# Squares of the low-rank inputs summed tile by tile, rotary tables made in the linear attention, x fetched ahead of the second weights

## The chip, the core and the metric

One core of a Trainium2 chip runs the whole kernel. Its engines are TensorE (PE, with PEld for the loading of its stationary operand), VectorE (DVE), ScalarE (ACT), GpSimd (POOL) and SyncE (SP), which issues most transfers. The metric is the device time of one execution in microseconds, the median of several runs. Smaller is better.

## The reference

A decoder block on x of 1024 tokens by 1024 channels, in float32. One normalised input feeds one wide projection; its parts go to two branches, multi-head latent attention (8 heads, rotary part of 32 channels) and gated linear attention (4 heads, chunks), which are gated, merged and projected back.

```python
h = rmsnorm(x, g_in[l])
proj = h @ w_in[l]
(c_q, c_kv, k_r, z_mla, q_g, k_g, v_g, a_lr, z_gla, gate_mla, gate_gla) = jnp.split(proj, split_points, axis=-1)
q = (rmsnorm(c_q, g_q[l]) @ w_uq[l]).reshape(B, S, MLA_HEADS, MLA_QK)
q = jnp.concatenate([q[..., :MLA_NOPE], apply_rope(q[..., MLA_NOPE:], cos, sin)], axis=-1)
kv = (rmsnorm(c_kv, g_kv[l]) @ w_ukv[l]).reshape(B, S, MLA_HEADS, MLA_NOPE + MLA_VDIM)
k_rope = apply_rope(k_r[:, :, None, :], cos, sin)
o_mla = mla_attention(q, k, v_mla).reshape(B, S, MLA_WIDTH)
log_a = jax.nn.log_sigmoid((a_lr @ w_gla_gate[l] + b_gla_gate[l]).astype(jnp.float32)) / GLA_GATE_NORM
o_gla = gla_chunked(q_g, k_g, v_g, log_a)
merged = jax.nn.sigmoid(gate_mla) * y_mla + jax.nn.sigmoid(gate_gla) * y_gla
x = x + merged @ w_out[l]
return rmsnorm(x, g_final)
```

The low-rank inputs are c_kv (256 channels, two tiles of 128) and c_q (384, three tiles). Their normalisation needs the sum of the squares over all channels of each token. The rotary tables are the sines and cosines of position times frequency.

## The kernel before

The tokens are done in two halves of 512. A half goes through four stages: the start with the low-rank inputs (the latent stage), the linear attention, the latent attention, and the merge with the output products. To keep float32 accuracy each operand is split in a high and a low part, and each product of tiles is three matmuls: high by high, high by low, low by high.

The weights of a half are a stream of units (class Stream). A unit is one tile of 128 output columns: 24 matmuls of 128 x 128 by 128 x 512, written as a generator that yields behind each six. For each unit a weight of 512 KB is loaded (load_raw, two buffers), cast to its high part by ScalarE, and its low part is made by VectorE or GpSimd (split_raw, three buffers each). ahead() loads LOAD_AHEAD = 2 weights and splits SPLIT_AHEAD = 3 ahead of use. step(n) advances the stream by n yields; upto(name) runs it through a unit; ride(chain) runs other work and advances the stream by what that work yields, so that matmuls of units lie between its steps. The units of a half begin with misc (the gate's rank-16 input and the rotary key), ckv0, ckv1, cq0, cq1, cq2, then q0, k0, v0, z0, z1 and so on for four heads.

The order of each engine's instructions is made by a planner from a simulated run: what stands first in the code has precedence, but an engine that is idle gets any later instruction whose inputs and buffers are ready. Transfers on SyncE's queue are ordered in the same way, and at run time an engine takes its instructions strictly in the planned order.

The start of the first half (h == 0): eleven products of zeros (NWARM, tile zw), the first weight in two pieces, x tile 0, then st.ahead() (the next weights), then the prologue's x tiles 1 to 3 (xs, each 512 KB with two k-tiles: xh by ScalarE, xl by VectorE), the constants, and x again by rows (xr), whose squares ScalarE sums for the row scales rcol (POOL makes the power, L252). bcast_row (L257) turns a column of scales into a row by eight small matmuls.

In the latent stage four chains lie over the units. decay() makes the gate: stk from krr, four products with wgs (L693) into two banks, on each an Abs of ScalarE (L694) and a minimum of VectorE (L695), then Exp and Ln over all, then sums along the tokens with the row rst. latent() for ckv and cq: each latent unit ends with a square into csq and a copy into craw (L326, L327); when all tiles are there, matmuls of two columns with one2 add the squares over the channels (L715, 8 for ckv and 12 for cq in each half, two records each in the trace), and from these come the scales. tables() (L665 to L680) makes the sines and cosines into um[:, 2:4], and rotate(krr, ...) turns the rotary key (L627 to L630). In the code tables() stands behind unit cq2 and the rotation behind latent_q. csq has a single buffer, as has each of the banks tr, at and ups; ops has two, and the units' results three.

## Time and profile before

| | us |
|---|---|
| median of 3 runs (1082.48 to 1083.81) | 1083.74 |
| the profiled execution | 1085.81 |
| its span in the trace | 1084.0 |
| outside the span | 1.81 |
| TensorE busy, share of the span | 1048.3, 97% |
| VectorE, ScalarE, GpSimd busy | 714.0, 542.1, 374.9 |
| granted clock of TensorE, mean | 0.98 |

The page's chain of work that ended last gives TensorE 77% of the span, VectorE 12%, ScalarE 4%. Matmuls are pipelined: a product of 512 columns is shown with some 0.4 us, while the next one starts earlier, so a busy TensorE need not be one at its best; the spacing of starts and the granted clock tell that. The granted clock is 1.00 at 2.4 GHz and 0.50 at 1.2 GHz. In the waits, the name behind the arrow is the instruction that came last.

### The profile page before, as it was taken

Reading aid. Unit: us, or ns where it says so; the run is one execution under the profiler, and the core shown is the slowest. Engines: PE = TensorE matmul, PEld = TensorE weight load, DVE = VectorE, ACT = ScalarE, POOL = GpSimd, SP = SyncE. Lnnn points to the kernel's source line nnn. Section 1 sums busy time; section 2 is a strip of 40 time slices with the busy share of each in tenths; the row PEclk is TensorE's granted clock in tenths of the full one; section 3 lists DMA queues with packets and bytes.
Section 4 is the critical chain, followed back from the end, with each engine's and each line's share of the span. In section 5 each row is a group of like instructions: output and inputs, shape, how many; then the busy total and the mean of one; then the engine's idle time right before and its main releaser. Section 6 shows DMA issues by size and latency. Waiting matters only on the chain.

```text
span 1084.0 us, 14078 instructions
## 1 busy us (share of the span) xinstructions
PE 1048.3 (97%) x5231; PEld 872.4 (80%) x5231; DVE 714.0 (66%) x1114; ACT 542.1 (50%) x910; POOL 374.9 (35%) x274
## 2 busy tenths in 40 slices
PE   8999999999999989999999999999999998999997
PEld 5798998987778867888889989988777776788875
DVE  5796555557586776466887655455767877667673
ACT  5744334455556653444574444344664656553232
POOL 2361121114445542230524211104454656533420
PEclk8899999999999999999999999999999999899999
DMA  8213213235433446644412233235422223424532
GB/s 297 98 59 97 97 60 117 97 100 195 139 98 111 144 139 250 226 138 144 165 60 78 78 102 101 80 112 158 122 96 70 81 83 121 125 90 161 175 111 98
DMA packets 46118, 132.05 MB, mean 122 GB/s; under 512 B 5232, under 2 KB 7664, under 8 KB 45920
## 3 DMA queue, kind: packets, MB, share of 16 engines
q1 hardware_dynamic: 37760, 113.96, 32.1%
q0 software_dynamic: 3680, 8.78, 3.0%
q10 hardware_dynamic: 4608, 8.39, 2.1%
q8 instruction: 41, 0.67, 0.3%
q14 instruction: 29, 0.24, 0.1%
HBM read 110.01 MB, written 21.10 MB: 121 GB/s over the span
## 4 chain that ended last, share of the span: by engine, by line
PE 77%; DVE 12%; ACT 4%; issue 2%; DMA 2%; POOL 1%; SPq 0%; POOLq 0%; DVEq 0%; ACTq 0%
PE pj L201 58%; DVE pl L943 2%; PE y L548 2%; PE y L546 2%; PE y L547 2%; PE ops L201 2%; DVE mx L893 1%; PE sc L930 1%; PE sc L932 1%; PE sc L933 1%; PE ov L951 1%; PE ov L952 1%; PE sc L886 1%; PE at L201 1%; DVE wlo L188 1%
## 5 line engine op out<-in xcount | busy, mean ns | idle before, releaser
L201 PE MATMUL pj<-xl,whi 128*128 128x512 f32 x800 | 301.0, 399 | 1.4 <-DVE xl L282 1.4
L201 PE MATMUL pj<-xh,whi 128*128 128x512 f32 x672 | 270.5, 403 | 2.4 <-ACT whi L187 1.6
L187 ACT CAST whi<-wraw 128x1024 fp32r<-128x1024 f32 (+1 forms) x151 | 155.3, 1029 | 122.0 <-PE pj L201 91.3
L201 PEld LDWEIGHTS pj<-xl,whi 128*128 128x128 f32 x800 | 153.5, 192 | 31.9 <-DVE xl L282 2.9
L201 PE MATMUL pj<-xh,wlo 128*128 128x512 f32 x672 | 176.6, 397 | 0.0
L188 POOL TENSOR_TENSOR wlo<-wraw,whi 128x1024 fp32r<-128x1024 f32 (+2 forms) x52 | 118.2, 2274 | 140.8 <-ACT whi L187 67.4
L201 PEld LDWEIGHTS pj<-xh,whi 128*128 128x128 f32 x672 | 129.7, 193 | 28.0 <-ACT whi L187 1.9
L201 PEld LDWEIGHTS pj<-xh,wlo 128*128 128x128 f32 x672 | 127.2, 191 | 26.3
L188 DVE TENSOR_TENSOR wlo<-wraw,whi 128x1024 fp32r<-128x1024 f32 x100 | 127.4, 1275 | 21.5 <-ACT whi L187 21.3
L945 POOL TENSOR_TENSOR acc<-acc,p 128x512 f32<-128x512 f32 (+3 forms) x80 | 84.9, 1061 | 86.0 <-ACT p L939 70.5
L943 DVE TENSOR_TENSOR pl<-p,ph 128x512 fp32r<-128x512 f32 (+3 forms) x80 | 70.3, 886 | 23.4 <-ACT ph L942 23.2
L939 ACT ACTIVATE p<-sc 128x512 f32<-128x512 f32 (+3 forms) x80 | 37.3, 468 | 68.8 <-DVE sc L935 50.8
L201 PE MATMUL pj<-wlo,xh 128*128 128x256 f32 x256 | 64.4, 285 | 0.0
L201 PE MATMUL pj<-whi,xh 128*128 128x256 f32 x256 | 64.2, 284 | 0.0
L893 DVE TENSOR_REDUCE mx<-sc 128x1 f32<-128x512 f32 (+2 forms) x96 | 51.8, 551 | 11.6 <-PE sc L886 10.4
L548 PE MATMUL y<-whi,zl 128*128 128x512 f32 x128 | 50.5, 396 | 0.5 <-DVE zl L211 0.5
L547 PE MATMUL y<-wlo,zh 128*128 128x512 f32 x128 | 50.4, 395 | 0.0
L546 PE MATMUL y<-whi,zh 128*128 128x512 f32 x128 | 49.5, 396 | 0.0
L201 PEld LDWEIGHTS pj<-wlo,xh 128*128 128x128 f32 x256 | 49.0, 191 | 0.3
L201 PEld LDWEIGHTS pj<-whi,xh 128*128 128x128 f32 x256 | 48.9, 191 | 0.3
L211 POOL TENSOR_TENSOR ql<-qi,qh 128x512 fp32r<-128x512 f32 x8 | 12.4, 1554 | 93.5 <-ACT qh L210 93.5
L349 DVE TENSOR_TENSOR zr<-pj,rbc 128x512 f32<-128x512 f32 x32 | 22.0, 688 | 33.8 <-PE pj L201 33.5
(298 smaller groups left out, 2101.6 us busy)
## 6 DMA issues: line engine op xcount, KB each, us to landing
wraw<-in_dram SPq DMA_DIRECT2D x141, 512.0 KB, 3.5
gtd<-zr ACTq DMA_DIRECT2D x32, 256.0 KB, 2.2
zr<-gtd SPq DMA_DIRECT2D x32, 256.0 KB, 2.9
xr<-in_dram SPq DMA_DIRECT2D x8, 512.0 KB, 9.4
ugd<-uo SPq DMA_DIRECT2D x16, 256.0 KB, 2.2
...
```

The costliest lines, as they stand in the source:

```text
L187: nc.scalar.copy(out=hi[:, 0:n], in_=raw[:, 0:n])
L188: getattr(nc, lo_engine).tensor_tensor(out=lo[:, 0:n], in0=raw[:, 0:n], in1=R(hi[:, 0:n]), op=ALU.subtract)
L201: nc.tensor.matmul(out=ps, lhsT=a, rhs=b, start=(i == 0), stop=(i == 3 * n - 1))
L211: (lo_engine or nc.vector).tensor_tensor(out=lo, in0=src, in1=R(hi), op=ALU.subtract)
L349: nc.vector.tensor_tensor(out=zr, in0=c.ps, in1=c.rbc, op=ALU.mult)
L546: nc.tensor.matmul(out=c.ops[t], lhsT=a[0], rhs=b[0], start=(k == 0), stop=False)
L547: nc.tensor.matmul(out=c.ops[t], lhsT=a[0], rhs=b[1], start=False, stop=False)
L548: nc.tensor.matmul(out=c.ops[t], lhsT=a[1], rhs=b[0], start=False, stop=(k == 7))
L893: nc.vector.reduce_max(mx[:, t, b:b + 1], ps[:, 0:n], axis=mybir.AxisListType.X)
L939: nc.scalar.activation(p[:, 0:n], ps[:, 0:n], AF.Exp, scale=SCALE)
L943: nc.vector.tensor_tensor(out=pl[:, 0:n], in0=p[:, 0:n], in1=R(ph[:, 0:n]), op=ALU.subtract)
L945: nc.gpsimd.tensor_tensor(out=s.acc[:, q0:TH], in0=s.acc[:, q0:TH], in1=p[:, 0:n], op=ALU.add)
```

## The change

Five things are changed. (1) The matmuls that add squares (four for each tile) are now put in a list, and issued tile by tile within the next latent unit, behind 18 of its 24 products; what is left is issued in latent(). ckv's sums use the bank ups, cq's the bank at. (2) tables() is a generator; its steps and the rotation of krr are taken one at each yield of the first three heads' linear attention. Its buffers are now parts of um. (3) In the first half's start only the first weight is split, x tiles 1 and 2 are fetched, and then the next weights follow. (4) In unit misc of the first half six products of zeros, of 512 columns, stand behind the fourth, sixth, ... fourteenth product. (5) wgs and rst lie in the pool of the linear attention: wgs is written to memory in the first half and read back in the second, rst is loaded in each half; the raw constants share one buffer.

```diff
--- before.py
+++ after.py
@@ -214,13 +214,15 @@
     vecs = mk(cst, [P, NVEC], F32, "vecs")
     nc.sync.dma_start(out=vecs, in_=vec)
 
+    def move(out, in_, queue=None):
+
+        (queue or nc.sync).dma_start(out=out.bitcast(F32), in_=in_.bitcast(F32))
+
     def vcol(base, i=0):
         return vecs[:, base + i:base + i + 1]
 
     idn = mk(cst, [P, P], F32, "idn")
     idr = mk(cst, [P, P], F32R, "idr")
-    wgs = mk(cst, [P, 512], F32R, "wgs")
-    rst = mk(cst, [P, TH], F32, "rst")
     msk = mk(cst, [P, 3, P], F32, "msk")
     onh = mk(cst, [P, 256], F32R, "onh")
     spr = mk(cst, [48, 4, P], F32R, "spr")
@@ -238,6 +240,7 @@
     junk = mk(cst, [P, 512], BF16, "junk")
     gst = [mk(cst, [P, 256], F32, f"gst{g}") for g in range(4)]
 
+    wgd = dram.tile([96, 512], F32R, tag="wgd", name="wgd")
     ugd = dram.tile([8, P, TH], F32, tag="ugd", name="ugd")
     gtd = dram.tile([16, P, TH], F32, tag="gtd", name="gtd")
     vsp = dram.tile([P, 4, HEADS, P], F32R, tag="vsp", name="vsp")
@@ -311,20 +314,49 @@
 
         @unit("misc", wunit(U_MISC), "vector")
         def _(w):
-            yield from proj(c, w)
+            if h == 0:
+                c.ps = mk(pj, [P, TH], F32, "pj")
+                todo = []
+                for k in range(KT):
+                    todo += [(w[0][:, k, :], c.xh[:, k, :]), (w[0][:, k, :], c.xl[:, k, :])]
+                todo += [(w[1][:, k, :], c.xh[:, k, :]) for k in range(KT)]
+                for i, (a, b) in enumerate(todo):
+                    mm = nc.tensor.matmul(out=c.ps, lhsT=a, rhs=b, start=(i == 0), stop=(i == 23))
+                    if i % 2 == 1 and 1 < i < 14:
+                        with tc.issue_after(mm.ins):
+                            nc.tensor.matmul(out=c.zp, lhsT=c.zw[:, 0:P], rhs=c.zw, start=True, stop=True)
+                    if i % 6 == 5 and i < 23:
+                        yield
+            else:
+                yield from proj(c, w)
             c.misc = c.ps
 
-        c.craw = {}
+        c.craw, c.cps, c.sums = {}, {}, {"ckv": [], "cq": []}
 
         def latent_unit(tag, i, u0):
             @unit(f"{tag}{i}", wunit(u0 + i), "gpsimd")
             def _(w):
-                yield from proj(c, w)
+                for n, _ in enumerate(proj(c, w)):
+                    if n == 2:
+                        for todo in c.sums.values():
+                            while todo:
+                                todo.pop(0)()
+                    yield
                 if i == 0:
-                    c.craw[tag] = (mk(c.pp, [P, 3, TH], F32, "craw" + tag), mk(c.pp, [P, 3, TH], F32, "csq"))
+                    c.craw[tag] = (mk(c.pp, [P, 2 if tag == "ckv" else 3, TH], F32, "craw" + tag), mk(c.pp, [P, 3, TH], F32, "csq"))
                 raw, sq = c.craw[tag]
                 nc.scalar.activation(sq[:, i, :], c.ps, AF.Square)
                 nc.scalar.copy(out=raw[:, i, :], in_=c.ps)
+
+                def add():
+                    if i == 0:
+                        c.cps[tag] = mk(c.gps, [P, TH], F32, "at" if tag == "cq" else "ups")
+                    last = i == (1 if tag == "ckv" else 2)
+                    for t in range(4):
+                        nc.tensor.matmul(out=c.cps[tag][:, 2 * t:2 * t + 2], lhsT=sq[:, i, t * P:(t + 1) * P], rhs=one2,
+                                         start=(i == 0 and t == 0), stop=last, skip_group_check=True)
+
+                c.sums[tag].append(add)
 
         for i in range(2):
             latent_unit("ckv", i, U_CKV)
@@ -590,22 +622,22 @@
         st.fences |= {f"{h}{u}" for u in ("misc", "uqr", "hi0", "hi1", "hi2", "hi3", "yg0", "ym0", "wo00")}
 
 
-    def consts(bp):
+    def consts(bp, wgs):
         graw = mk(bp, [P, 512], F32, "graw")
         nc.sync.dma_start(out=idn, in_=idn_d)
         nc.sync.dma_start(out=graw[0:96], in_=wgate)
         nc.scalar.copy(out=wgs[0:96, :], in_=graw[0:96])
         nc.vector.tensor_tensor(out=wgs[64:96, :], in0=graw[64:96], in1=R(wgs[64:96, :]), op=ALU.subtract)
+        move(wgd, wgs[0:96])
         nc.vector.tensor_scalar(out=ggh, in0=vecs[:, V_GGLA:V_GGLA + 2], scalar1=0.5, scalar2=None, op0=ALU.mult)
 
     def consts2(bp):
-        nc.sync.dma_start(out=rst, in_=rst_d)
         nc.sync.dma_start(out=msk, in_=msk_d)
         nc.vector.tensor_copy(out=idr, in_=idn)
-        oraw = mk(bp, [P, 256], F32, "onraw")
+        oraw = mk(bp, [P, 512], F32, "graw")[:, 0:256]
         nc.sync.dma_start(out=oraw, in_=onh_d)
         nc.vector.tensor_copy(out=onh, in_=oraw)
-        sraw = mk(bp, [48, 4, P], F32, "sraw")
+        sraw = mk(bp, [P, 512], F32, "graw")[0:48].rearrange("p (a b) -> p a b", a=4)
         nc.sync.dma_start(out=sraw, in_=spread_d)
         nc.vector.tensor_copy(out=spr, in_=sraw)
 
@@ -616,14 +648,40 @@
         gs = hs.enter_context(ExitStack())
         c.gp = gp = pool("gla", 1, stack=gs)
         c.gp2 = gp2 = pool("gla2", 2, stack=gs)
-        gps = pool("glaps", 1, PSUM, stack=gs)
+        c.gps = gps = pool("glaps", 1, PSUM, stack=gs)
+        wgs = mk(gp, [P, 512], F32R, "wgs")
+        rst = mk(gp, [P, TH], F32, "rst")
         um = mk(up, [P, 4, TH], F32, "um")
         sn, cn = um[:, 2, :], um[:, 3, :]
         krr = mk(up, [P, TH], F32, "krr")
 
-        def rotate(raw, rows):
-
-            sw = mk(c.pp, [P, TH], F32, "sw")
+        def tables():
+
+            ang, pi, tn = um[:, 0, :], um[:, 1, :].bitcast(I32), cn
+            nc.sync.dma_start(out=pi, in_=pos[:, h * TH:(h + 1) * TH].broadcast_to([P, TH]))
+            yield
+            nc.vector.tensor_copy(out=ang, in_=pi)
+            nc.vector.tensor_scalar(out=ang, in0=ang, scalar1=vcol(V_FREQ), scalar2=None, op0=ALU.mult)
+            yield
+            nc.vector.tensor_scalar(out=tn, in0=ang, scalar1=INV2PI, scalar2=MAGIC, op0=ALU.mult, op1=ALU.add)
+            nc.vector.tensor_scalar(out=tn, in0=tn, scalar1=MAGIC, scalar2=None, op0=ALU.subtract)
+            yield
+            for cc in (C1, C2, C3):
+                nc.vector.scalar_tensor_tensor(out=ang, in0=tn, scalar=-cc, in1=ang, op0=ALU.mult, op1=ALU.add)
+                yield
+            nc.vector.tensor_scalar(out=ang, in0=ang, scalar1=PI_CLAMP, scalar2=-PI_CLAMP, op0=ALU.min, op1=ALU.max)
+            nc.vector.scalar_tensor_tensor(out=tn, in0=ang, scalar=-1.0, in1=ang, op0=ALU.mult, op1=ALU.max)
+            yield
+            nc.scalar.activation(sn, ang, AF.Sin, scale=vcol(V_SGN))
+            nc.scalar.activation(cn, tn, AF.Sin, scale=-1.0, bias=hpi)
+            yield
+            rotate(krr, slice(96, 128), um[:, 1, :])
+            yield
+
+        def rotate(raw, rows, sw=None):
+
+            if sw is None:
+                sw = mk(c.pp, [P, TH], F32, "sw")
             nc.vector.stream_shuffle(out=sw[rows], in_=raw[rows], mask=[(i + 16) % 32 for i in range(32)])
             nc.vector.tensor_tensor(out=sw[rows], in0=sw[rows], in1=sn[rows], op=ALU.mult)
             nc.vector.tensor_tensor(out=raw[rows], in0=raw[rows], in1=cn[rows], op=ALU.mult)
@@ -636,9 +694,9 @@
             if h == 0:
                 with ExitStack() as bs:
                     bp = pool("boot", 1, stack=bs)
-                    zw = mk(bp, [P, TH], BF16, "zw")
+                    c.zw = zw = mk(gp, [P, TH], BF16, "zw")
                     nc.vector.memset(zw, 0.0)
-                    zp = mk(gps, [P, TH], F32, "tr")
+                    c.zp = zp = mk(gps, [P, TH], F32, "tr")
                     for _ in range(NWARM):
                         nc.tensor.matmul(out=zp, lhsT=zw[:, 0:P], rhs=zw, start=True, stop=True)
                     pro = prologue(0, bp, 4)
@@ -646,38 +704,26 @@
                     st.nload = 1
                     next(pro)
                     load_rest(st.raw[0], st.specs[0][0])
-                    for _ in range(NB):
+                    st.LOAD_AHEAD, st.SPLIT_AHEAD = 0, 1
+                    st.ahead()
+                    st.LOAD_AHEAD, st.SPLIT_AHEAD = Stream.LOAD_AHEAD, Stream.SPLIT_AHEAD
+                    for _ in range(3):
                         next(pro)
                     st.ahead()
-                    for _ in range(4 - NB):
-                        next(pro)
-                    consts(bp)
+                    next(pro)
+                    consts(bp, wgs)
                     for _ in pro:
                         pass
                     consts2(bp)
+            if h == 1:
+                move(wgs[0:96], wgd)
+            nc.sync.dma_start(out=rst, in_=rst_d)
             c.pp = pp = pool("start", 1, stack=ss)
             st.upto(f"{h}misc")
             st.step(NBS[h])
             bps = mk(gps, [P, TH], F32, "tr")
             bcast_row(c.rcol, c.rbc, bps)
             nc.vector.tensor_tensor(out=krr, in0=c.misc, in1=c.rbc, op=ALU.mult)
-
-            def tables():
-
-                pi = mk(pp, [P, TH], I32, "pi")
-                nc.sync.dma_start(out=pi, in_=pos[:, h * TH:(h + 1) * TH].broadcast_to([P, TH]))
-                ang = mk(pp, [P, TH], F32, "ang")
-                nc.vector.tensor_copy(out=ang, in_=pi)
-                nc.vector.tensor_scalar(out=ang, in0=ang, scalar1=vcol(V_FREQ), scalar2=None, op0=ALU.mult)
-                tn = mk(pp, [P, TH], F32, "tn")
-                nc.vector.tensor_scalar(out=tn, in0=ang, scalar1=INV2PI, scalar2=MAGIC, op0=ALU.mult, op1=ALU.add)
-                nc.vector.tensor_scalar(out=tn, in0=tn, scalar1=MAGIC, scalar2=None, op0=ALU.subtract)
-                for cc in (C1, C2, C3):
-                    nc.vector.scalar_tensor_tensor(out=ang, in0=tn, scalar=-cc, in1=ang, op0=ALU.mult, op1=ALU.add)
-                nc.vector.tensor_scalar(out=ang, in0=ang, scalar1=PI_CLAMP, scalar2=-PI_CLAMP, op0=ALU.min, op1=ALU.max)
-                nc.vector.scalar_tensor_tensor(out=tn, in0=ang, scalar=-1.0, in1=ang, op0=ALU.mult, op1=ALU.max)
-                nc.scalar.activation(sn, ang, AF.Sin, scale=vcol(V_SGN))
-                nc.scalar.activation(cn, tn, AF.Sin, scale=-1.0, bias=hpi)
 
             def decay():
 
@@ -709,11 +755,10 @@
                 hi = mk(lat, [P, n, TH], F32R, "chi" + tag)
                 lo = mk(lat, [P, n, TH], F32R, "clo" + tag)
                 yield 3
-                cps = mk(gps, [P, TH], F32, "at")
-                for t in range(4):
-                    for i in range(n):
-                        nc.tensor.matmul(out=cps[:, 2 * t:2 * t + 2], lhsT=sq[:, i, t * P:(t + 1) * P], rhs=one2,
-                                         start=(i == 0), stop=(i == n - 1))
+                full = "c" + ("kv" if tag == "k" else "q")
+                while c.sums[full]:
+                    c.sums[full].pop(0)()
+                cps = c.cps[full]
                 f1 = mk(pp, [P, 4], F32, "f1" + tag)
                 nc.vector.tensor_tensor(out=f1, in0=c.rcol, in1=c.rcol, op=ALU.mult)
                 f2 = mk(pp, [P, 4], F32, "f2" + tag)
@@ -741,9 +786,7 @@
             st.upto(f"{h}ckv1")
             st.ride(latent_kv())
             st.upto(f"{h}cq2")
-            tables()
             st.ride(latent_q())
-            rotate(krr, slice(96, 128))
 
 
         with ExitStack() as gs2:
@@ -834,9 +877,15 @@
                     nc.sync.dma_start(out=ugd[f], in_=uo)
                     yield 1
 
+            side = tables()
             for g in range(4):
                 st.upto(f"{h}v{g}")
-                st.ride(core(g))
+                for n in core(g):
+                    st.step(n)
+                    if g < 3:
+                        next(side, None)
+            for _ in side:
+                pass
         gs.close()
```

## Rows read from the trace of the kernel before

**Rows 1.** Windows: busy us (instructions) of each engine, then granted clock, DMA share, GB/s.
```profile
6.00:10.90 4.90, 2.74 (x8) 1.38 (x9) 2.94 (x5) 2.57 (x5) 0.98 (x1) 1.00 0.92 359
...
10.90:17.75 6.85, 6.01 (x14) 4.23 (x14) 6.08 (x8) 5.86 (x10) 1.40 (x1) 0.50 1.04 371
...
41.60:48.50 6.90, 6.32 (x17) 5.16 (x18) 4.07 (x8) 5.47 (x7) 1.02 (x1) 0.51 0.42 152
...
62.10:65.50 3.40, 3.40 (x10) 2.62 (x9) 3.40 (x5) 0.21 (x2) 2.74 (x2) 0.50 0.29 113
...
80.00:120.00 40.00, 40.00 (x250) 35.94 (x249) 24.20 (x40) 17.13 (x35) 8.57 (x7) 1.00 0.24 79
...
560.90:563.90 3.00, 1.97 (x18) 1.92 (x18) 3.00 (x7) 3.00 (x7) 0.89 (x1) 1.00 0.00 0
...
563.90:570.70 6.80, 6.80 (x20) 5.45 (x20) 6.49 (x11) 2.46 (x6) 5.69 (x5) 0.50 0.24 80
```

**Rows 2.** Timeline of TensorE, start: start us, us, engine, line, instruction, [wait before].
```profile
1.30 3.91 PE L643 MATMUL tr<-zw 128*128 128x512 bf16 x11 [1.30 <-DVE zw L640]
...
9.89 0.50 PE L201 MATMUL pj<-xh,whi 128*128 128x512 f32 x1 [1.55 <-ACT whi L187]
...
12.90 0.79 PE L201 MATMUL pj<-xl,whi 128*128 128x512 f32 x1 [0.84 <-DVE xl L282]
...
23.93 1.05 PE L257 MATMUL tr<-idn,rcol 128*128 128x128 f32 x8
...
24.74 0.48 PE L201 MATMUL pj<-xh,whi 128*128 128x512 f32 x1
```

**Rows 3.** Timeline of ScalarE and GpSimd, start.
```profile
8.80 1.04 ACT L187 CAST whi<-wraw 128x1024 fp32r<-128x1024 f32 x1 [2.09 <-DMA wraw<-in_dram]
...
10.08 2.61 ACT L281 ACTIVATE xh<-xs,vecs 128x512 fp32r<-128x512 f32 x4 [0.24 <-DMA xs<-in_dram]
...
13.14 1.34 ACT L281 ACTIVATE xh<-xs,vecs 128x512 fp32r<-128x512 f32 x2 [0.45 <-DMA xs<-in_dram]
...
20.54 1.05 ACT L187 CAST whi<-wraw 128x1024 fp32r<-128x1024 f32 x1 [0.16 <-DMA wraw<-in_dram]
...
20.66 1.02 POOL L252 TENSOR_TENSOR rcol<-ms,mhalf 128x4 f32<-128x4 f32 x1 [8.36 <-DVE ms L251]
```

**Rows 4.** Timeline of TensorE, latent stage of both halves.
```profile
34.66 1.98 PE L201 MATMUL pj<-xh,wlo 128*128 128x512 f32 x8
...
42.18 0.80 PE L693 MATMUL ops<-stk,wgs 96*128 96x512 f32 x1 [1.58 <-DVE mn L695]
...
45.34 3.45 PE L201 MATMUL pj<-xh,wlo 128*128 128x512 f32 x8
...
59.11 2.73 PE L715 MATMUL at<-one,csq 128*128 128x2 f32 x24
...
64.08 0.63 PE L201 MATMUL pj<-xh,whi 128*128 128x512 f32 x1
...
561.98 2.73 PE L715 MATMUL at<-one,csq 128*128 128x2 f32 x20 [1.03 <-ACT csq L326]
```

**Rows 5.** Timeline of VectorE and ScalarE, latent stage of both halves.
```profile
26.40 0.74 DVE L627 STREAM_SHUFFLE sw<-krr 32x512 f32<-32x512 f32 x1
...
27.64 2.65 DVE L671 TENSOR_SCALAR ang<-ang,vecs 128x512 f32<-128x512 f32 x1
...
30.74 0.60 ACT L326 ACTIVATE csq<-pj 128x512 f32<-128x512 f32 x1 [1.76 <-PE pj L201]
...
31.84 1.28 ACT L679 ACT_TABLE_LOAD   x1
...
36.68 0.73 ACT L679 ACTIVATE um<-ang,vecs 128x512 f32<-128x512 f32 x1 [3.56 <-DVE ang L677]
...
43.72 0.60 ACT L326 ACTIVATE csq<-pj 128x512 f32<-128x512 f32 x1
...
533.83 0.49 DVE L671 TENSOR_SCALAR ang<-ang,vecs 128x512 f32<-128x512 f32 x1
```

## The prediction

> **What bounds the kernel now.** I read three views, in this order. First the windows over the first 120 us and over the same stage of the second half [rows 1]. In the linear attention TensorE is busy throughout (40.00 of 40 us in 80 to 120) at full clock, so nothing can be won there. Four places are otherwise: the start, with the clock at half (1.2 of 2.4 GHz) from 10.9 to 17.75; 41.6 to 48.5 us; 62.1 to 65.5 us; and 560.9 to 570.7 us. Behind the start, all lie in the latent stage of a half (the units ckv, cq and the first q unit), and the change touches both. Second, TensorE's timeline in these places [rows 2, 4]: it shows what TensorE did before the clock fell. Third, the other engines' rows there [rows 3, 5]: which wait ends last.
>
> Two spacings carry the sums. Eight products at full clock take 1.98 us (34.66, [rows 4]), the last one's own 0.4 us included (the page's mean for one is 399 ns), so one comes every (1.98 - 0.4)/7 = 0.23 us. At half clock eight take 3.45 us (45.34), with 0.6 for the last (64.08 has 0.63): (3.45 - 0.6)/7 = 0.41. Each product at half clock loses 0.18 us. Eight tiny products of the rotation of a column to a row (L257) take 1.05 us [rows 2]; 24 records of the sums of squares take 2.73 us [rows 4], 0.114 each.
>
> **The start.** From the first real product, at the start of the window of 6.0 us [rows 1], to the first of ckv1 at 24.74 [rows 2] TensorE does misc and ckv0, 48 products: 48 x 0.23 + 1.05 = 12.1 us of work in 18.7 us, so 6.6 us are lost. Why: product 9.89 waits for the cast of the second weights and 12.90 for the low part of x [rows 2]. The second weights land at 8.80, and only then the next x tile, at about 10.08, and the last at 13.14 [rows 3]. The transfers are of one size, 512 KB, and land one behind the other: with tiles 1 and 2 (of 0 to 3) ahead of the weights each comes 10.08 - 8.80 = 1.3 us earlier; tile 3 keeps its place; the weights come two places later, at 8.80 + 2.6 = 11.4, and their cast (1.04) ends at 12.5. That is hidden as long as the twelve products of the first three x tile pairs and the zero products fill the time. The six zero products cost 6 x 0.23 to 6 x 0.41 = 1.4 to 2.5 us of TensorE, but fall where it waits (1.55 + 0.84 us in the two marked waits, and gaps beside them). Zero operands do count as work for the clock: eleven of them from 1.30 [rows 2] were all that TensorE had done ahead of the full clock of 6.0 to 10.9 [rows 1]. If they keep the clock up in 10.9 to 17.75, 14 records x 0.18 = 2.5 us come back; if it falls all the same, about half of it, as the products then come closer together. The upper end is set by others: the third weights' cast ends at 20.54 + 1.05 = 21.6 and the column of row scales, which L257 needs, at 20.66 + 1.02 = 21.7 [rows 3]; ckv1 can't start before, so at most 24.74 - 21.7 = 3.0 us. The lower end is a loss of 1 us (zero products at half clock with no wait to hide them: four of six behind 10.9, 4 x 0.41 = 1.6, less half of what x brings). I take 1.5 us, nearer the middle, since three chains (clock, scales, weights) must all be in time for more.
>
> **The sums of squares.** The count stays: 20 small matmuls a half (two records each), 40 x 0.114 = 4.6 us. What goes is the clump. From 24.74 to the first product of unit k0 at 64.08 [rows 2, 4] there are 39.3 us. Work: five units, 120 x 0.23 = 27.6; sums 4.6; four gate products (L693) 4 x 0.23 = 0.9; L257 1.05; together 34.2. Lost: 5.1 us, and 0.8 more behind 64.08 while the clock is still low. The rows say where: the gate product at 42.18 waited 1.58 us for VectorE [rows 4]; 17 records at half clock from 41.6, some 12 of them full products, lose 12 x 0.18 = 2.2; ten records from 62.1 lose 1.8 [rows 1]. Both falls of the clock stand right behind a clump: the sums of ckv around the wait, and the 24 records of cq at 59.11 [rows 4]. In the second half, 20 records stand in one clump, 1.03 us of waiting for the last square ahead of it [rows 4], and the clock is at half for 6.8 us with 20 records, 15 of them full products: 15 x 0.18 = 2.7 [rows 1]. Lost there: 3.7 us. Put behind 18 of the 24 products of the next unit, four matmuls (8 x 0.114 = 0.9 us) stand between full products. Also, the buffer of squares is single, so the square of cq0 came only at 43.72 [rows 5], when the ckv sums were through, 7.1 us behind its last product (34.66 + 1.98 = 36.6, [rows 4]); with the sums early the buffer comes free in time. What is late next: a group of sums that waits in TensorE's queue holds all products behind it, until ScalarE has made its square. From the unit's last product ScalarE has 18 x 0.23 = 4.1 us for that; the square of 30.74 waited for TensorE itself [rows 5], so it is in time unless ScalarE is held up.
>
> **The tables.** Eight VectorE operations of [128 x 512] at 0.43 to 0.69 us (estimated: L671's 0.49 where GpSimd was quiet, [rows 5], and the page's 688 ns for a form with two tensors, L349), four for the rotation at 0.74 or less, two sines of 0.73, one table load of 1.28 us [rows 5], and the fetch of the positions on SyncE's queue. The new place in the code is not a new time. The planner of the instruction order gives an idle engine whatever is ready: the shuffle of krr ran at 26.40 [rows 5], though its code stands behind the latents' last step. So in the first half I expect the tables to be drawn forward again; but their input now goes to a buffer that waits for nobody, and in the second half to one that is free since the first half's merge, so they can run during the output products, where they meet no decay chain. What counts is what they block. Now ScalarE stands 3.56 us before the first sine because VectorE is late [rows 5]: L671 took 2.65 us beside GpSimd's splits and 0.49 us in the second half without [rows 5]. Behind the sine stand the gate's Abs steps, which free the banks for which 42.18 waits. With lower priority they block less. If they do run in the linear attention, VectorE has room (24.20 of 40 us busy in 80 to 120, [rows 1]), but TensorE's cover there is complete, and any wait shows at once. Bounds: nothing, to the sines and the load on the path once in each half, 2 x (2 x 0.73 + 1.28) = 5.5 us; I take 0.8, near nothing, as VectorE and ScalarE are idle for over a third of that stretch.
>
> A rule speaks against this part. The Trainium skill (ScalarE: Activation LUTs, "Table sets: the hidden batching unit") says to do all calls of one set together, since each change of set loads a table, and gives 2.66 us with the drain. The trace has the load alone at 1.28 us [rows 5]. With one load more on the path in each half the sum would be, by the page's figure, 5.3 us worse; by the row 2.6 (rival d).
>
> **The rest.** The gate weights go out to memory and come back for the second half, the reset row is loaded twice, two constants share one buffer: 0.2 to 0.3 MB each on SyncE's queue. The store makes SyncE wait for the split gate weights, the shared buffer for VectorE's casts; weights of the latents are queued behind. Three weights are split ahead of their use, and a unit takes 24 x 0.23 = 5.5 us, which covers it; so I put it at nothing. Without that cover it is the 3.5 us that a weight takes to land (the page's list of transfers), once: 0 to 3.5 in the range.
>
> **Sum.** Start 1.5; first latent stage 5.1 + 0.8 lost, of which I give back 5.0, since other stretches of the kernel keep some waiting too; second 3.7, of which 3.5 come back; less 0.8: 9.2 us. The profiled execution took 1085.81 us with a span of 1084.0 (1.81 outside) and lies 2.1 above the median, 1083.74. I take the gain from the median: 1074.5 us; on the profiled execution it would be 1076.6.
>
> **Rivals.** (a) The sums spread and the clock holds, but the tables are planned into the same place and ScalarE blocks the gate as now, and the start gives nothing. For it: 26.40. Against it: the new buffers. First latent stage then gives 3, the second 3, the rest -0.5: 1083.7 - 5.5 = 1078.2. (b) It doesn't do what it says: the planner puts the sums where it finds TensorE idle, or they become late again, and the clock still falls in each place, only elsewhere. For it: the order is planned and not written. Against it: the sums are ready early and have precedence over the products behind them. 1083 +- 1.5. (c) Slower: the squares come late. Each of the eight groups inside a running unit then holds TensorE's queue. For it: cq0's square, 7.1 us behind [rows 4, 5]. Against it: that one waited for sums which now come early. It decides from a mean lateness of 4.1 + 9.2/8 = 5.3 us. Were four of the eight as late as cq0's, it costs 4 x (7.1 - 4.1) = 12.0: 1083.7 - 9.2 + 12.0 = 1086.5. (d) The sines run between the exponentials of the linear attention, and each half pays a load more on the path, 2 x 1.28 = 2.6 us [rows 5]: 1077.1. Against it: ScalarE is busy 17.13 of 40 us there [rows 1], so it would seldom be last. It is of this case that the Trainium skill's page on ScalarE warns.
>
> **How the numbers follow.** Forecast (1070 to 1078) 0.58; (a) 0.16; (d) 0.04; (b) 0.12; (c) 0.10. 0.2% is 2.2 us, about what a measurement of this kernel can tell from no change. Faster: 0.58 + 0.16 + 0.04 = 0.78; same 0.12 (b); slower 0.10. The range 1067.5 to 1082.5 takes in the forecast with both ends of its unknown costs (start 3.0 instead of 1.5 and every loss given back; the tables 5.5 and a late weight 3.5), (a), (d) and some of (b); it leaves out (c), the rest of (b), and a gain from order elsewhere.
>
> **What would show it.** Right: no clump of sums over 8 records; clock 1.00 from 24 to 80 us and around 565; k0's first product near 57 (64.08 - 1.5 - 5); no wait of TensorE for VectorE near 42. Wrong: TensorE waiting for squares inside a unit; the half clock still there at 11 to 17; SyncE waiting for VectorE ahead of weights; new waits of TensorE between 80 and 240 us; a ScalarE table load between the linear attention's exponentials.

## The result, and the profile after

The changed kernel takes 1088.36 us (median of 6 runs, 1086.11 to 1089.76) against 1082.01 for the kernel before (6 runs, 1080.93 to 1083.81): ratio 1.0056, 95% interval 1.0040 to 1.0072. It is 6 us slower; 1074.5 was forecast, with a range up to 1082.5. Executions of one kernel lie some us apart (before: 1077.9 to 1086.5 in all runs of this study), and the profiled one of before, 1085.81, lies high among them; so below gains and losses are read from medians, and from traces distances inside a stage. One run of all those below, one of e7 (1139 us), fell in a slower state of the chip and is left out of its ratio.

Windows of the kernel after, the stretches of [rows 1] and three more (columns as there):

```profile
10.90:17.75 6.85, 6.85 (x26) 4.63 (x25) 4.88 (x7) 5.45 (x9) 2.38 (x1) 0.83 1.04 358
41.60:48.50 6.90, 5.53 (x33) 4.55 (x32) 3.32 (x7) 2.59 (x4) 1.16 (x2) 1.00 0.43 152
62.10:65.50 3.40, 3.40 (x17) 2.81 (x16) 3.40 (x3) 0.74 (x1) 2.23 (x2) 1.00 0.00 0
...
560.90:563.90 3.00, 3.00 (x15) 2.46 (x14) 3.00 (x4) 0.52 (x1) 0.00 (x0) 1.00 0.47 175
563.90:570.70 6.80, 6.72 (x34) 5.41 (x33) 6.80 (x10) 3.35 (x7) 4.24 (x3) 1.00 0.01 2
...
9.90:13.30 3.40, 3.29 (x8) 1.68 (x7) 2.52 (x4) 2.65 (x4) 0.67 (x1) 0.50 1.05 346
71.30:78.10 6.80, 4.83 (x22) 4.86 (x23) 5.80 (x12) 3.80 (x7) 4.33 (x3) 0.50 0.18 65
572.00:580.00 8.00, 5.99 (x44) 5.50 (x43) 6.63 (x9) 4.36 (x7) 4.53 (x4) 1.00 0.42 143
```

The reader sees that what the change was to do was done in the latent stages: full clock in the three places there of [rows 1]. The half clock of the start is shorter, 9.9 to 13.3, but that this comes from the change is not shown: e18 below, whose start is that of the kernel before, had full clock in the same window (TensorE's busy time, clock, DMA share, GB/s):

```profile
10.90:17.75 6.85, 5.62 (x25) 1.00 1.04 368
```

So the half clock at the start belongs to some executions of that start and not to others; the prediction had one of the first kind. In the latent stage TensorE is now idle for 2.0 us of 71.3 to 78.1, at half clock there, and for 2.0 us of 572 to 580. Its timeline names the waits:

```profile
58.04 1.05 PE L356 MATMUL at<-one,csq 128*128 128x2 f32 x8 [0.86 <-ACT csq L348]
...
60.44 0.40 PE L201 MATMUL pj<-xh,whi 128*128 128x512 f32 x1
...
69.76 0.39 PE L201 MATMUL pj<-wlo,xh 128*128 128x256 f32 x1 [2.63 <-DVE wlo L188]
...
73.27 2.04 PE L260 MATMUL tr<-idn,f3q 128*128 128x128 f32 x8 [3.01 <-DVE f3q L769]
...
577.11 1.13 PE L260 MATMUL tr<-idn,f3q 128*128 128x128 f32 x8 [2.01 <-DVE f3q L769]
```

k0 begins at 60.44, 3.6 us before its time of [rows 4]. Ten us later all of it is gone: TensorE stands 2.63 us for the low part of v0's weights and 3.01 us for f3q, the scale column of cq, which L260 turns into a row; in the second half 2.01 us for the same column. Both come from VectorE. These are the two rows of before that the prediction did not read (VectorE's f3q, TensorE's L257, in each half):

```profile
67.36 1.18 DVE L724 TENSOR_TENSOR f3q<-f3q,rcol 128x4 f32<-128x4 f32 x1
...
69.12 1.05 PE L257 MATMUL tr<-idn,f3q 128*128 128x128 f32 x8
...
570.40 1.25 DVE L724 TENSOR_TENSOR f3q<-f3q,rcol 128x4 f32<-128x4 f32 x1
...
573.44 1.05 PE L257 MATMUL tr<-idn,f3q 128*128 128x128 f32 x8
```

The column was ready at 68.55 and TensorE came for it at 69.12; in the second half 571.65 and 573.44. So TensorE had, in this execution, only 0.6 and 1.8 us to gain before it met VectorE: 2.4 of the 8.5 that the prediction gave back. And in the kernel after the column is later still. What stands ahead of it, on VectorE and ScalarE:

```profile
22.67 1.92 DVE L663 CAST um<-um 128x512 f32<-128x512 int32 x1 [1.80 <-DMA um<-in_dram]
...
28.70 4.21 DVE L670 SCALAR_TENSOR_TENSOR um<-um 128x512 f32<-128x512 f32 x3
32.84 0.41 DVE L642 CAST spr<-graw 48x512 fp32r<-48x512 f32 x1
...
34.37 0.68 DVE L732 TENSOR_TENSOR stk<-krr,stk 32x512 fp32r<-32x512 f32 x1
...
68.29 0.15 DVE L765 TENSOR_TENSOR f2q<-at,f1q 128x4 f32<-128x4 f32 x1
...
72.97 0.16 DVE L769 TENSOR_TENSOR f3q<-f3q,rcol 128x4 f32<-128x4 f32 x1
```

```profile
33.34 0.60 ACT L348 ACTIVATE csq<-pj 128x512 f32<-128x512 f32 x1 [3.14 <-DVE spr L642]
...
35.41 1.28 ACT L675 ACT_TABLE_LOAD   x1
...
39.83 1.26 ACT L740 ACTIVATE S<-ops,vecs 128x512 f32<-128x512 f32 x2
...
46.36 1.05 ACT L187 CAST whi<-wraw 128x1024 fp32r<-128x1024 f32 x1 [4.31 <-DMA wraw<-in_dram]
47.31 1.26 ACT L740 ACTIVATE S<-ops,vecs 128x512 f32<-128x512 f32 x2
48.59 1.28 ACT L744 ACT_TABLE_LOAD   x1
49.88 1.92 ACT L744 ACTIVATE S<-S 128x2048 f32<-128x2048 f32 x1
...
458.03 1.28 ACT L675 ACT_TABLE_LOAD   x1 [3.23 <-DVE um L672]
```

In the first half the tables stand in the latent stage still, now ahead of the gate's split (L732, done at 35.05). In the second half they have left it, as the prediction expected: their sines run at 458 us, in the first half's output products. ScalarE waits for a constant, runs the sines, then stands 4.31 us for a weight, and behind that, in its order, are the gate's second pair of Abs steps and the exponentials. The scans follow, and f2q (its sums were complete at 59) comes behind them at 68.29.

### The profile page after: what moved, and what is told of

Read it like the earlier page. It is cut to its first block, busy times and chain, and to the rows that moved or that the text cites. A ratio compares the mean times of both kernels' runs of the same rounds, so it can differ in the third digit from the quotient of the medians.

```text
span 1088.0 us, 14105 instructions
## 1 busy us (share of the span) xinstructions
PE 1046.6 (96%) x5237; PEld 870.0 (80%) x5237; DVE 709.7 (65%) x1114; ACT 542.0 (50%) x910; POOL 374.5 (34%) x274
## 4 chain that ended last, share of the span: by engine, by line
PE 69%; DVE 14%; ACT 5%; DMA 5%; issue 3%; POOL 2%; SPq 0%; POOLq 0%; DVEq 0%; ACTq 0%
PE pj L201 52%; DVE pl L992 2%; PE ops L201 2%; DVE wlo L188 2%; DMA zr<-gtd 2%; PE y L580 2%; PE y L578 2%; PE y L579 2%; DVE mx L942 1%; PE sc L979 1%; DMA zr<-ugd 1%; PE sc L981 1%; PE sc L982 1%; DVE zl L211 1%; PE ov L1001 1%
## 5 line engine op out<-in xcount | busy, mean ns | idle before, releaser
L201 PE MATMUL pj<-xl,whi 128*128 128x512 f32 x792 | 293.8, 394 | 0.0
L201 PE MATMUL pj<-xh,whi 128*128 128x512 f32 x664 | 263.6, 397 | 0.0
L201 PEld LDWEIGHTS pj<-xl,whi 128*128 128x128 f32 x792 | 149.8, 189 | 27.9
L201 PE MATMUL pj<-xh,wlo 128*128 128x512 f32 x664 | 171.1, 392 | 0.0
L201 PEld LDWEIGHTS pj<-xh,whi 128*128 128x128 f32 x664 | 125.6, 189 | 23.5
L201 PEld LDWEIGHTS pj<-xh,wlo 128*128 128x128 f32 x664 | 123.8, 188 | 25.5
```

Source lines behind the costliest of these rows:

```text
L201: nc.tensor.matmul(out=ps, lhsT=a, rhs=b, start=(i == 0), stop=(i == 3 * n - 1))
```

## The experiments

All times are medians with their own runs of before beside them (1081.6 to 1082.8); the ratio is to those. Three theories: (S) the shared constants' buffer, (T) the tables in the latent stage, (V) TensorE, early through the spread sums, meets VectorE's column.

| kernel | us | ratio, 95% interval |
|---|---|---|
| e1 changed, own constants' buffers | 1087.95 | 1.0051, 1.0034 to 1.0068 |
| e2 changed, tables held | 1076.93 | 0.9956, 0.9938 to 0.9974 |
| e3 both | 1077.97 | 0.9960, 0.9940 to 0.9980 |
| e4 before + sums | 1083.86 | 1.0011, 0.9994 to 1.0029 |
| e5 before + start | 1081.97 | 0.9990, 0.9974 to 1.0007 |
| e6 before + tables, held | 1076.74 | 0.9944, 0.9928 to 0.9961 |
| e7 e4 + late row | 1079.19 | 0.9963, 0.9949 to 0.9977 |
| e8 e2 + late row | 1074.20 | 0.9916, 0.9898 to 0.9933 |
| e9 before + tables as written | 1081.33 | 0.9984, 0.9970 to 0.9998 |
| e10 changed, tables behind the gate's split | 1085.81 | 1.0033, 1.0018 to 1.0048 |
| e11 before + start, sums, held tables, late row | 1073.43 | 0.9915, 0.9892 to 0.9937 |
| e12 before + buffers | 1085.86 | 1.0030, 1.0013 to 1.0048 |
| e13 changed, only the sines held | 1080.62 | 0.9987, 0.9973 to 1.0000 |
| e14 changed, without the buffers | 1081.20 | 0.9989, 0.9975 to 1.0004 |
| e15 e12, own constants' buffers | 1086.57 | 1.0036, 1.0021 to 1.0052 |
| e16 before + store of the gate weights | 1082.76 | 1.0009, 0.9999 to 1.0019 |
| e17 before + second load of the reset row | 1081.85 | 0.9999, 0.9986 to 1.0012 |
| e18 before + late row | 1081.02 | 0.9989, 0.9977 to 1.0002 |

**e1, the shared buffer undone.**

```diff
-        oraw = mk(bp, [P, 512], F32, "graw")[:, 0:256]
+        oraw = mk(bp, [P, 256], F32, "onraw")
...
-        sraw = mk(bp, [P, 512], F32, "graw")[0:48].rearrange("p (a b) -> p a b", a=4)
+        sraw = mk(bp, [48, 4, P], F32, "sraw")
```

> The changed kernel with one edit: the two constants (one-hot rows and spread rows) have buffers of their own again, as in the kernel before. Three theories. (S) The shared buffer is the cause: its chain (cast of the one-hot rows, transfer of the spread rows, their cast) held SyncE for 4.1 us ahead of weights and the square of ckv0 for 3.14 us. Then SyncE's and ScalarE's waits go, k0 comes some 3 to 4 us earlier and the time is near 1084 (changed kernel: 1088.4). (T) The tables, drawn ahead of the gate on VectorE, are the cause: most of them are still ahead of it, so the time stays at 1087 to 1089. (V) The sums are early but TensorE then waits for VectorE's queue (column scale of cq, split weights) where there was cover before: 2.6 and 3.0 us of waiting near 70 to 73 us stay, and the time stays at 1087 to 1089.

No change. SyncE's wait for the one-hot rows' cast went (4.1 us in the changed kernel), the gate's split ended at 33.87 instead of 35.05, and yet f3q was ready at 73.13, the same as without the edit (from the start of krr, the scaled result of unit misc, 46.9 us for 48.1); TensorE waited 4.3 us for v0's weights. (S) falls for the shared buffer.

**e2, the tables held in the linear attention; e3, with e1's edit too.** Only the order on VectorE is bound (issue_after: not ahead of the marked instruction); `c.mark` is the masking step `at` of `core`:

```diff
-            nc.vector.tensor_copy(out=ang, in_=pi)
+            with tc.issue_after(c.mark.ins):
+                nc.vector.tensor_copy(out=ang, in_=pi)
```

> The changed kernel with one edit: the first operation of the rotary tables on VectorE may not be ordered before the masking step of the linear attention's first head pair; all others follow it by their data. (T) Then VectorE's split of the gate input comes about 3 us earlier, the exponentials and scans with it, and the time is near 1084. (S) The shared buffer still holds SyncE and the squares: 1087 to 1089. (V) If the scans come earlier, the column scale of cq comes earlier as well, and part of the 5.6 us of waiting near 70 to 73 us goes: 1084 to 1086; if it stays, 1087 to 1089. If the sines land between exponentials, table loads are added: up to 2 x 1.28 us back.

> Both edits: buffers of their own for the two constants, and the tables not before the linear attention. (S) and (T) together: each undoes its own part, 1078 to 1081, which is under the kernel before (1082.0). (S) alone: as with the buffers alone, near 1084. (T) alone: as with the pinned tables alone, near 1084. (V): the waits of TensorE for the column scale of cq and the split weights remain in part, 1085 to 1088.

11 us faster than the changed kernel (1.0056 to 0.9956 of 1082), more than (T) had expected; e3 adds nothing. ScalarE's table loads and the sines of e2, and TensorE's last wait:

```profile
47.20 1.28 ACT L746 ACT_TABLE_LOAD   x1
...
56.62 1.28 ACT L402 ACT_TABLE_LOAD   x1
...
92.22 1.28 ACT L676 ACT_TABLE_LOAD   x1
93.52 0.73 ACT L676 ACTIVATE um<-um,vecs 128x512 f32<-128x512 f32 x1
94.15 0.71 ACT L677 ACTIVATE um<-um,hpi 128x512 f32<-128x512 f32 x1
94.88 1.28 ACT L371 ACT_TABLE_LOAD   x1
```

```profile
66.72 1.13 PE L260 MATMUL tr<-idn,f3q 128*128 128x128 f32 x8 [2.16 <-DVE f3q L770]
```

```profile
80.00:120.00 40.00, 40.00 (x249) 35.94 (x248) 32.39 (x56) 21.21 (x39) 7.11 (x5) 1.00 0.27 88
```

Two table loads instead of four stand in the first half's latent stage; the two that came into the linear attention cost TensorE nothing that shows, as it is busy for 40.00 of its 40 us (third fence: windows of e2, 80 to 120 us). TensorE still waits 2.16 us for f3q.

**e4, the sums alone on the kernel before** (the change's `latent_unit` and `add`, and in `latent`):

```diff
-                for t in range(4):
-                    for i in range(n):
-                        nc.tensor.matmul(out=cps[:, 2 * t:2 * t + 2], ...
+                while c.sums[full]:
+                    c.sums[full].pop(0)()
```

> The kernel before with one part of the change alone: the squares are summed tile by tile inside the next unit. By the prediction the clumps and their half clock go from both latent stages, 8.5 us: 1073 to 1075. (S) and (T) put the loss on other parts of the change, so the gain must show here: 1074 to 1078. (V) What the clumps no longer cost is lost to waits for VectorE's column scale of cq, in the first half 5 us, in the second 2 us: 1081 to 1086, no better than the kernel before.

(V) holds, the prediction's 8.5 us are not there. TensorE's two rows say why, and two of VectorE:

```profile
68.23 2.05 PE L257 MATMUL tr<-idn,f3q 128*128 128x128 f32 x8 [3.88 <-DVE f3q L738]
...
574.63 1.21 PE L257 MATMUL tr<-idn,f3q 128*128 128x128 f32 x8 [2.01 <-DVE f3q L738]
```

```profile
570.19 1.23 DVE L188 TENSOR_TENSOR wlo<-wraw,whi 128x1024 fp32r<-128x1024 f32 x1 [0.16 <-ACT whi L187]
571.33 0.15 DVE L734 TENSOR_TENSOR f2q<-at,f1q 128x4 f32<-128x4 f32 x1
```

TensorE arrives early, waits 3.88 us and has done L257 45.5 us behind the start of krr; before it had in 44.5. In the second half it is 47.4 for 46.8. There the column slipped too: f2q, its first step, stands behind a weight's split that in the kernel before follows it.

**e5, the start alone** (with the change's first unit, zero products and all, and ckv's raw tile two wide):

```diff
+                    st.LOAD_AHEAD, st.SPLIT_AHEAD = 0, 1
+                    st.ahead()
+                    st.LOAD_AHEAD, st.SPLIT_AHEAD = Stream.LOAD_AHEAD, Stream.SPLIT_AHEAD
-                    for _ in range(NB):
+                    for _ in range(3):
                         next(pro)
                     st.ahead()
```

> The kernel before with the start of the change alone: x tiles 1 and 2 fetched ahead of the second weights, six zero products between the first unit's products (and the raw tile of ckv two wide, to make room for the zero tile). By the prediction 1.5 us faster: 1081.0. By the changed kernel's trace, where ckv1 began 1.0 us earlier and the first rotary row 0.6 us: 1081.5 to 1082. Rival: the gain is lost by the end of the latent stage, since that stage then waits for the same VectorE step: 1082.5.

1.1 us by the ratio, with no change inside the interval: about as forecast, but not told from none. In its trace the clock is full from the first product to 41 us, as in e18 without the edit, and krr starts at 23.73 us, in e18 at 23.98. TensorE then waits 0.3 us at L257 for VectorE; start and column end together.

**e6, the tables alone, held** (e2's edit, the change's `tables` and `side` on the kernel before):

```diff
             st.upto(f"{h}cq2")
-            tables()
             st.ride(latent_q())
-            rotate(krr, slice(96, 128))
...
+                for n in core(g):
+                    st.step(n)
+                    if g < 3:
+                        next(side, None)
```

> The kernel before with the tables alone moved into the linear attention and held there (not before the masking of the first head pair). (T) VectorE's queue of the latent stage is what is late there: without the 5 to 6 us of tables in it, the wait near 42 us (1.58) and the half clock behind it (2.2) go: 1078.5 to 1080.5, while the clump of the cq sums and its half clock stay. Rival, that tables count only when the sums are early, since with late sums TensorE never comes to the cq scale too soon: 1081.5 to 1083.

(T) holds beyond its own number: 6.1 us, two thirds of the best kernel's gain, with the sums untouched. f3q is ready at 62.41 us, 38.1 behind krr where before it took 42.9; TensorE, at 63.39, is now the later one.

**e7, e4 with the row of cq's scale later; e8, e2 with it; e18, before with it.**

```diff
-                yield 3
+                yield 3 if tag == "k" else 9
                 fb = mk(pp, [P, TH], F32, "fb")
```

> The kernel with the sums alone (1083.9), with one edit more: the four matmuls that turn cq's scale column into a row stand nine steps of the products behind it and not three. Nothing reads that row before the attention. (V) The wait of 3.88 us for the cq scale goes, the half clock behind it too (some 2 us), and in the second half 2 us of waiting: 1076 to 1078; the prediction's gain by the spread sums is there, and had only been taken back by this wait. Rival: TensorE meets the next thing that VectorE delivers late (split weights, the keys' decay) and the time stays at 1081 to 1084.

> The changed kernel with the tables held in the linear attention (1076.9), and the row of cq's scale made nine steps behind its column instead of three. (V) The remaining wait of 2.16 us in the first half and 0.7 in the second go: 1073.5 to 1075. Rival: another wait for VectorE takes its place: 1076 to 1077.

> The kernel before with the row of cq's scale nine steps behind its column instead of three, and nothing else. In the trace of before TensorE came 0.57 us behind the scale in the first half and 1.79 us in the second, so it waited for nothing there: if the spread sums are what gains and the late row only uncovers it, 1081.5 to 1082.5. If the late row gains by itself, as in the run with both: 1079.

The row alone gives nothing (e18: no change inside the interval). With the sums it gives 5 us (1.0011 to 0.9963), and with held tables 4 (0.9956 to 0.9916). So the spread sums are worth something, but only where TensorE need not wait for f3q. Even then e7 is 4 us faster than before, under half of the 8.5, and missed its own forecast (1076 to 1078). In its trace a smaller wait took the place of the first:

```profile
67.78 0.39 PE L201 MATMUL pj<-wlo,xh 128*128 128x256 f32 x1 [1.93 <-DVE wlo L188]
...
72.56 1.05 PE L257 MATMUL tr<-idn,f3q 128*128 128x128 f32 x8
```

**e9, the tables alone as the change writes them** (e6 without the hold), **e10, the changed kernel with the hold at the gate's split** instead of the masking step:

```diff
-                nc.vector.tensor_tensor(out=stk[32:64], ...
+                c.mark = nc.vector.tensor_tensor(out=stk[32:64], ...
```

> The kernel before with the tables alone moved as the change writes them: their code stands in the linear attention, but nothing holds them there. Held there, they gave 1076.7 against 1082.7 of before. (T) The order of the instructions is planned, the positions' buffer is free at once, and in the first half the tables come into VectorE's queue of the latent stage again, two operations and the shuffle ahead of the gate's split: no gain there, only what the second half gives (3 us with the held tables): 1080 to 1084. Rival: the place in the code is enough: 1077 to 1079, and then the changed kernel's loss is in the meeting of parts.

> The changed kernel with the tables held only behind VectorE's split of the gate's input (not in the linear attention). If what costs is that seven table operations stand ahead of that split, the time is near that with the tables held in the linear attention: 1077 to 1079. If what costs is that they are in the latent stage at all, VectorE's queue and ScalarE's two sines with their table load ahead of the exponentials, most of the loss stays: 1084 to 1088.

Without the hold 1.7 us of e6's 6.1 are left, and they lie in the second half, where the tables moved to the output products: from krr to f3q it is 41.9 us for 43.9 before, in the first half 42.6 for 42.9. Putting the tables behind the gate's split gives 2.5 of e2's 11. That does not settle what the place ahead of the split costs, since the hold has a second effect: the second half's tables, at 458 us in the changed kernel, are drawn into the latent stage by it (e10, ScalarE):

```profile
534.80 1.28 ACT L676 ACT_TABLE_LOAD   x1
```

From krr to f3q the first half gains 3.8 us by the hold (48.1 to 44.3; e2 gains 6.7), the second loses 2.0 (44.6 to 46.6).

**e13, the changed kernel with only the two sines held**, on ScalarE, behind the copy `ath` of `core`:

```diff
-                split(ath, atl, at, nc.gpsimd)
+                c.mark = nc.scalar.copy(out=ath, in_=at)
+                nc.gpsimd.tensor_tensor(out=atl, in0=at, in1=R(ath), op=ALU.subtract)
...
+            with tc.issue_after(c.mark.ins):
                 nc.scalar.activation(sn, ang, AF.Sin, scale=vcol(V_SGN))
                 nc.scalar.activation(cn, tn, AF.Sin, scale=-1.0, bias=hpi)
```

> The changed kernel with the two sines alone held on ScalarE behind the first head pair of the linear attention; the tables' VectorE operations stay where the plan puts them, seven of them ahead of the gate's split. If ScalarE is what costs (sines and table loads ahead of the Abs steps and the exponentials: 2 x 0.73 + 2 x 1.28 = 4.0 us), the time is near that with all tables held: 1077 to 1080. If VectorE's queue ahead of the gate's split is what costs: 1084 to 1088.

7.5 us back (1.0056 to 0.9987), just above the range expected: ScalarE carries about two thirds of what e2 gained. Seven table operations still stand between krr and the gate's split (done at 34.95), yet the scans' subtraction `mn` starts at 50.66 instead of 56.11 us, and f3q is ready at 67.67. The rest, 3.4 us to e2, is put down to VectorE's table operations by subtraction.

**e12, the buffers alone; e15, without the sharing; e16 and e17, one edit each; e14, the changed kernel without the buffers.** e12 is this, with the shared buffer; e15 takes e1's edit; e16 has the lines on `wgs` alone, e17 those on `rst` alone.

```diff
-    wgs = mk(cst, [P, 512], F32R, "wgs")
-    rst = mk(cst, [P, TH], F32, "rst")
...
+        move(wgd, wgs[0:96])
...
+        wgs = mk(gp, [P, 512], F32R, "wgs")
+        rst = mk(gp, [P, TH], F32, "rst")
...
+            if h == 1:
+                move(wgs[0:96], wgd)
+            nc.sync.dma_start(out=rst, in_=rst_d)
```

> The kernel before with the rest of the change alone: two constants through one shared buffer, the gate weights stored and fetched again for the second half, the reset row loaded in each half. By the prediction nothing, 0 to 3.5 us: 1082 to 1086, with 1082.7 the likeliest. (S) The chain through the shared buffer delays weights and squares: 1085 to 1087.

> The kernel with the buffers alone (1085.9), but the two constants with buffers of their own; the store of the gate weights and the second reset row stay. If the wait of 4.09 us in VectorE's queue for the second constant is what cost there: 1082 to 1083, like the kernel before. If it is the store or the reset row: 1085 to 1087.

> The kernel before with one buffer edit alone: the gate weights are stored and fetched again for the second half. If this is what cost in the run of the buffers with own constants (1086.6): 1085 to 1087. If it is the reset row: 1082.

> The kernel before with one buffer edit alone: the reset row is loaded in each half, behind the constants. If this is what cost in the run of the buffers with own constants (1086.6): 1085 to 1087. If it is the store: 1082. If each costs half: 1084 in both.

> The whole change without its buffers: the start, the sums tile by tile and the tables as the change writes them, on the kernel before; the two constants with buffers of their own, gate weights and reset row kept for both halves. If the loss is the sum of parts, start (-0.8), sums (+1.3) and tables as written (-0.6) make 1082; if the buffers' 3.3 us are all that is missing, the changed kernel's 1088 less 3.3, 1085. If the loss is in the meeting of early sums and tables in the latent stage, 1086 to 1088.

The buffers cost 3.2 us alone and 7 in the change (e14 to the changed kernel). Where the tables are held no cost shows (e8 and e11 agree, 0.9916 and 0.9915, give or take 3 us). Without the buffers the change is about the sum of its parts, as e14's first case said: 1.2 us faster than before, not told from no change. The rows of e12, VectorE and then TensorE:

```profile
29.77 2.13 DVE L613 CAST spr<-graw 48x512 fp32r<-48x512 f32 x1 [4.09 <-DMA graw<-in_dram]
```

```profile
67.14 0.39 PE L201 MATMUL pj<-wlo,xh 128*128 128x256 f32 x1 [1.90 <-DVE wlo L188]
...
70.55 2.05 PE L260 MATMUL tr<-idn,f3q 128*128 128x128 f32 x8 [2.55 <-DVE f3q L732]
...
573.25 2.05 PE L260 MATMUL tr<-idn,f3q 128*128 128x128 f32 x8 [3.34 <-DVE f3q L732]
```

VectorE stands 4.09 us for the second constant, the tables queue behind it, and f3q is ready 2.7 us later than before, counted from krr (45.6 for 42.9), in the second half 1.0 (44.9 for 43.9). But the sharing isn't needed for the loss: e15 is as slow, and store and reset row alone cost 0 to 1 us, so that e16 points at e17's edit and e17 at e16's, and neither by itself is the cost. In e15's trace f3q isn't late (41.4 and 43.7). Against e17, whose order in the latent stages is nearly the same, it loses 2.7 us between L257 (568.56 in e17, 568.71 in e15) and the linear attention's first transpose (`tr<-idn,ki`, 582.20 and 585.07), with TensorE's clock at half for 567.9 to 574.7 against 560.0 to 563.4. Which of the edits costs in company, and how, stays open.

In e14 ScalarE's rows, and one of TensorE in the changed kernel, show part of what the buffers change:

```profile
37.20 0.67 ACT L732 ACTIVATE S<-ops,vecs 128x512 f32<-128x512 f32 x1
...
41.79 1.29 ACT L732 ACTIVATE S<-ops,vecs 128x512 f32<-128x512 f32 x2
...
44.39 1.92 ACT L736 ACTIVATE S<-S 128x2048 f32<-128x2048 f32 x1
46.21 1.03 ACT L187 CAST whi<-wraw 128x1024 fp32r<-128x1024 f32 x1
```

```profile
44.26 0.50 PE L739 MATMUL ops<-stk,wgs 96*128 96x512 f32 x1
```

The same weight cast comes at the same time as in the changed kernel (46.21 and 46.36), but there the gate's second pair of Abs steps and the first exponential stand behind it (47.31 and 49.88), here ahead of it. So the planner's order, and not the transfer, made about half of these 5.5 us: the changed kernel's last gate product ends at 44.76, and its Abs steps could have started there instead of at 47.31. The other half was lost before, where the first pair stands behind both sines and two casts (39.83; in e14 from 37.20).

**e11, all that gains, without the buffers.**

> The kernel before with four parts: the start, the sums tile by tile, the tables held in the linear attention, and the row of cq's scale nine steps behind its column; without the shared buffer, the store of the gate weights and the second load of the reset row. Against the changed kernel with held tables and late row (1074.2): if these three cost nothing, as the prediction took it, 1073 to 1075; if they cost what (S) put on them, 3 us or more, 1070 to 1072.

The best kernel: 9.2 us faster than before by the ratio. That this is the prediction's number is chance, as two thirds of it come from holding the tables. Windows over both latent stages of e11 (busy time of TensorE alone, clock, DMA share, GB/s):

```profile
24.00:80.00 56.00, 56.00 (x333) 1.00 0.26 87
536.00:590.00 54.00, 54.00 (x318) 1.00 0.24 78
```

No wait and no half clock. The changed kernel has 48.13 at 0.94 and 51.91 at 1.00 there, the kernel before 54.42 at 0.91 and 52.84 at 0.94.

One table sums it up: when f3q is ready, counted from the start of krr, and how long after that TensorE's L257 (L260) starts; 0.15 is the least that occurs: TensorE was waiting. Each is one execution; up to f3q e5 and e18 have the latent stage of before, and show 42.2 and 42.0, then 43.9 and 43.8.

| kernel | first half: f3q, then TensorE | second half |
|---|---|---|
| before | 42.9, 0.57 | 43.9, 1.78 |
| changed | 48.1, 0.15 | 44.6, 0.15 |
| e4 sums | 43.3, 0.15 | 46.0, 0.15 |
| e12 buffers | 45.6, 0.15 | 44.9, 0.15 |
| e14 changed without buffers | 42.8, 0.15 | 44.6, 0.15 |
| e13 changed, sines held | 42.8, 0.15 | 43.0, 0.15 |
| e2 changed, tables held | 41.4, 0.15 | 43.0, 0.15 |
| e6 tables held | 38.1, 0.98 | 41.2, 1.24 |
| e8 e2 + late row | 41.4, 2.72 | 43.0, 3.88 |

The changed kernel's column is 5.2 and 0.7 us later than before's: 5.9, and the kernel is 6.1 slower. That the two come so close is partly luck. In e4 the column is 2.5 us later and 1.2 us are lost, in e6 it is 7.5 earlier and 6.1 are gained; and the kernels with part of the buffer edits don't fit: in e15 it is 1.8 us earlier, and 3.9 us are lost. So the column accounts for the tables and the sums, not for all that the buffers cost.

## Why the prediction was wrong

From the forecast, 9.2 us faster, to the result, 6.1 slower, are 15 us. Without the buffers the change gains 1.2 (e14): so 8 of the 15 are gain that was not there, and 7 are the buffers, which had been put at nothing.

- **The sums, 8.5 of its 9.2 us: this step failed.** The spacing, the work and TensorE's losses were read rightly for that execution, and k0 came 3.6 us earlier. The step "what is late next" named only the squares of ScalarE (0.86 us in the end). It didn't ask for the next thing that TensorE itself fetches from the chain beside it, though f3q and L257 stand in the trace of before 0.6 and 1.8 us apart. A loss of an engine can be given back only as far as the slack of what it meets next: 2.4 us here. Measured alone the sums are 1.2 us slower, not told from no change, as f3q also slipped by 2.1 us in the second half (e4); with the fetch moved later they gain 4 (e7), while moving the fetch by itself shows no gain (e18).
- **The tables, -0.8: the place was forecast rightly, the size was not.** That the first half's would be drawn forward again was forecast and came, and the second half's ran in the output products, as forecast; "with lower priority they block less" was wrong in the changed kernel. In the latent stage they cost 6.1 us already before the change (e6), and holding them out of the changed kernel gives 11. So the place in the code was worth 1.7 (e9), a gain where 0.8 of loss was put, and the place in time 6.1. The half that the prediction weighed, sines that block ScalarE, is the larger one (e13). It counted one table load a half for them; e2's stage lost two, since the exponentials behind the sines load theirs again. (Its eight operations on VectorE are nine, which changes none of its sums.)
- **The rule against this part.** With the sines held, each half has two table loads of 1.28 us between other functions in the linear attention (e2's rows), and TensorE doesn't feel them; the stage before has two fewer. The Trainium skill (ScalarE: Activation LUTs, "Table sets: the hidden batching unit") asks to batch calls by set. That going to the sines and back costs a load each way the trace bears out, but at 1.30 us from the load's start to the sine's (92.22, 93.52) and not the 2.66 that the prediction cites. But what counted was where the loads stood, not their number: behind the kernel's start it is eight in the kernel before, the changed one and e2, and ten in e11, the fastest.
- **The rest, taken at 0: failed.** Alone 3.2 us, in the change 7. The cover named, weights split ahead, is TensorE's. VectorE and ScalarE work in order, and what was queued behind the waits there were the tables and the gate's steps; that explains e12's column and part of the changed kernel's, and the rest of the cost stays open. That the shared buffer itself was to blame was my first theory, and fell (e1, e15).
- **The start, -1.5: within its bounds**, 1.1 (-0.8 to 2.8, e5), and so not told from none. Of the clock, its largest term, the runs show nothing either way: e5 has no half clock at the start, and e18, with the start of before, has none either.
- **Rivals.** (c) had the side and nearly the time, 1086.5, and the form, in-order TensorE waiting inside a unit; but for the squares, where it was the scale and a weight, so its number is luck. (a) saw that ScalarE would block the gate, without what follows. (b), the clock falling elsewhere, came in the first half (71.3 to 78.1), beside the wait for the scale. (d) priced sines in the linear attention at a loss of 2.6; there no loss shows.
- **Signs.** "Clock 1.00 around 565" came, and no clump of sums is over 8 records; "from 24 to 80" didn't (half at 71.3 to 78.1); a wait for VectorE near 42 stayed (1.37 us at 43.54, for `mn`); k0 "near 57" came at 60.44. Of the signs for wrong, a wait for squares inside a unit came (0.86 us), half clock in part of 11 to 17, and SyncE waiting for VectorE ahead of weights (4.1 us, ahead of the spread rows), which wasn't the cause. The upper bound, 1082.5, is 0.2 under the sum of its own terms (1074.5, 4.7 more for the tables, 3.5 for a late weight).
